# RMSNorm with doubled rows: wide squares, sums on VectorE, powers on GpSimd

## The chip, the cores and the metric

The kernel runs on one core of one Trainium2 chip. The metric is device microseconds of that core; a measurement is a median over several runs. Engines are named as in the profile: DVE is VectorE, ACT is ScalarE, POOL is GpSimd, SP is SyncE, which here only issues DMAs. Rows of the profile that end in q (SPq) belong to an engine's queue of waits and DMA issues.

## What is computed

```python
B, S, D = 8, 512, 2048
x_rep = np.repeat(x, 2, axis=1)
rms = np.sqrt((x_rep ** 2).mean(axis=-1, keepdims=True) + 1e-6)
out = ((x_rep / rms) * gamma[None, None, :]).astype(np.float32)
```

Each row of 2048 float32 numbers is divided by its root mean square, multiplied by gamma, and written twice. 33.56 MB are read and 67.11 MB written.

## The kernel before

The 4096 rows are cut into 8 tiles. A tile `y` has 128 partitions with K = 4 rows of x each, and room for 8 rows (R = 2 output rows for each row of x). The load puts the 4 rows of x into slots 4 to 7 of the tile; the results go in place into slots 0, 2, 4, 6, and copies of them into slots 1, 3, 5, 7. The store then writes all 8 slots, 64 KB for a partition. There are three buffers of this kind, so a load of tile 3 needs the store of tile 0 to be done, and so on.

Per row `k` of a tile, `square` (L64, L68) makes ScalarE square the row into PSUM with the row's sum in an accumulator, and take the root of its mean plus eps. `scale` (L73, L74) makes VectorE take the reciprocal and multiply row, reciprocal and the broadcast gamma in one instruction (scalar_tensor_tensor). After four rows `repeat` (L81) copies the first two results on ScalarE and the last two on VectorE, both at once 4096 elements wide.

The order is written out by hand: each engine runs its instructions in the order of the program. SP issues all loads (L52) and stores (L56) of tiles on one queue, in this order: load 0 in two halves, loads 1, 2; stores 0, 1, 2; loads 3, 4, 5; stores 3, 4; loads 6, 7; stores 5, 6, 7. The lines that set this:

```python
loads_after = {2: (3, 4, 5), 4: (6, 7)}
for i in range(ntiles):
    compute(i)
    store(i, 0, K)
    for j in loads_after.get(i, ()):
        load(j, nc.sync)
```

Gamma is read in seven pieces by ScalarE's queue (L95) into one partition, and GpSimd broadcasts it to all 128 (L96).

Of the kernel before, what the change touches and what calls it, by code (L numbers as in the profile page):

```python
# [1 line left out]

# [4 lines left out]


@with_exitstack
def kernel(  # L10
    ctx: ExitStack,
    tc: tile.TileContext,
    x: bass.AP,
    gamma: bass.AP,
    out: bass.AP,
):
    nc = tc.nc
    P = nc.NUM_PARTITIONS
    f32 = mybir.dt.float32
    Act = mybir.ActivationFunctionType  # L20
    Alu = mybir.AluOpType

    B, S, D = x.shape
    Bo, So, Do = out.shape
    R = So // S
    assert R == 2 and D == Do and B == Bo and So == S * R
    eps = 1e-6
    inv_d = 1.0 / float(D)


    K = 4
    N = B * S
    assert N % (P * K) == 0
    ntiles = N // (P * K)
    x_t = x.rearrange("b s d -> (b s) d").rearrange("(n p k) d -> n p k d", p=P, k=K)
    out_t = out.rearrange("b s d -> (b s) d").rearrange("(n p j) d -> n p (j d)", p=P, j=K * R)

    singles = ctx.enter_context(tc.tile_pool(name="singles", bufs=1))
    rows = ctx.enter_context(tc.tile_pool(name="rows", bufs=3))
    junk = ctx.enter_context(tc.tile_pool(name="junk", bufs=1, space=bass.MemoryType.PSUM))  # L40
    small = ctx.enter_context(tc.tile_pool(name="small", bufs=8))

    ys = []

    def load(i, eng, parts=1):


        y = rows.tile([P, K * R, D], f32, name="y")
        step = K // parts
        for k in range(0, K, step):  # L50
            at = K * (R - 1) + k
            eng.dma_start(out=y[:, at : at + step, :], in_=x_t[i, :, k : k + step, :])  # L52
        ys.append(y)

    def store(i, k0, k1):
        nc.sync.dma_start(  # L56
            out=out_t[i, :, R * k0 * D : R * k1 * D],
            in_=ys[i][:, R * k0 : R * k1, :].rearrange("p j d -> p (j d)"),
        )

    def square(i, k):
        sq = junk.tile([P, D], f32, name="sq")
        ss = small.tile([P, 1], f32, name="ss")
        nc.scalar.activation(  # L64
            out=sq[:], in_=ys[i][:, K * (R - 1) + k, :], func=Act.Square, accum_out=ss[:]
        )
        rms = small.tile([P, 1], f32, name="rms")
        nc.scalar.activation(out=rms[:], in_=ss[:], func=Act.Sqrt, scale=inv_d, bias=eps_t[:])  # L68
        return rms

    def scale(i, k, rms):
        rstd = small.tile([P, 1], f32, name="rstd")
        nc.vector.reciprocal(out=rstd[:], in_=rms[:])  # L73
        nc.vector.scalar_tensor_tensor(  # L74
            out=ys[i][:, R * k, :], in0=ys[i][:, K * (R - 1) + k, :], scalar=rstd[:], in1=gamma_b[:],
            op0=Alu.mult, op1=Alu.mult,
        )

    def repeat(i, k0, k1, copy):
        y_r = ys[i].rearrange("p (k r) d -> p k r d", r=R)  # L80
        copy(out=y_r[:, k0:k1, 1, :], in_=y_r[:, k0:k1, 0, :])  # L81

    def compute(i):
        for k in range(K):
            scale(i, k, square(i, k))
        repeat(i, 0, K // 2, nc.scalar.copy)
        repeat(i, K // 2, K, nc.vector.tensor_copy)


    ctx.enter_context(tc.manual_schedule())  # L90
    load(0, nc.sync, parts=2)
    gamma_b = singles.tile([P, D], f32, name="gamma_b")
    cuts = [0, *range(D // 4, D + 1, D // 8)]
    for c0, c1 in zip(cuts, cuts[1:]):
        nc.scalar.dma_start(out=gamma_b[0:1, c0:c1], in_=gamma[c0:c1].partition_broadcast(1))  # L95
    nc.gpsimd.partition_broadcast(out_ap=gamma_b[:], in_ap=gamma_b[0:1, :])  # L96
    eps_t = singles.tile([P, 1], f32, name="eps_t")
    nc.vector.memset(eps_t, eps)  # L98
    load(1, nc.sync)
    load(2, nc.sync)  # L100

    assert ntiles == 8
    loads_after = {2: (3, 4, 5), 4: (6, 7)}
    for i in range(ntiles):
        compute(i)
        store(i, 0, K)
        for j in loads_after.get(i, ()):
            load(j, nc.sync)  # L110


# [1 line left out]
_INS = ['x', 'gamma']  # L114
_OUTS = [((8, 1024, 2048), 'float32')]


# [23 lines left out]
```

## Time and profile before

| | |
|---|---|
| median of 3 runs | 239.44 us (239.32 to 239.5) |
| the profiled execution's own time | 239.72 us |
| its span, first to last instruction | 237.9 us |
| busy DVE / ACT / POOL | 96.5 / 101.0 / 2.5 us |
| main DMA queue q1 | 100.66 MB, 98.5% of 16 engines' span |
| DMA over the span | 423 GB/s |
| stores issued at | 27.05, 39.22, 51.39, 115.86, 128.25, 160.08, 184.02, 196.41 us |
| first x instruction of tiles 0, 3, 6 on ACT | 8.12, 101.18, 169.34 us |

Times in the trace are microseconds from the start of the span. A row of a group of instructions gives line, engine, operation, output<-input with partitions x elements and type, then xcount, then busy us, the mean ns of one instruction, and the idle time of the engine just before them with what ended most of it. A row of waits gives who waited for whom, us in total, how often, and the longest. A busy share of a DMA queue near 100% says that its 16 engines had packets all the time.

### The profile page before, as it was taken

The page shows a single profiled execution, that of the slowest core. Times are in us where ns is not written, and L with a number is a line of the kernel's source. Part 1 is how long each engine was busy: PE and PEld are TensorE (multiplying, and loading weights), DVE is VectorE, ACT ScalarE, POOL GpSimd, SP SyncE. Part 2 cuts the span into 40 slices and gives each one's busy share as a digit, 9 for nine tenths or more (in the row PEclk, how much of TensorE's full clock was granted, in tenths as well). Part 3 has the DMA queues.
Part 4 walks back from the last instruction along what each step waited for, and adds up shares of the span by engine and source line. Part 5 has one row for each costly group of instructions (what it writes and reads, how often), then busy time and mean ns, then how long its engine had stood idle before and what let it go on. Part 6 is the DMA issues. An engine that isn't in the chain of part 4 may idle for free.

```text
span 237.9 us, 287 instructions
## 1 busy us (share of the span) xinstructions
DVE 96.5 (41%) x73; ACT 101.0 (42%) x106; POOL 2.5 (1%) x5
## 2 busy tenths in 40 slices
DVE  0049999960000000059999960000199990000000
ACT  2697999900000000099999920000599960000000
POOL 0030000000000000000000000000000000000000
DMA  7999998989899998999998999989998989999994
GB/s 265 436 446 441 441 441 353 530 353 496 386 452 430 397 485 353 441 441 441 441 518 364 464 419 430 452 369 430 435 518 364 518 364 485 397 452 430 408 474 176
DMA packets 2464, 100.69 MB, mean 423 GB/s; under 512 B 279, under 2 KB 285, under 8 KB 286
## 3 DMA queue, kind: packets, MB, share of 16 engines
q1 hardware_dynamic: 2448, 100.66, 98.5%
q14 instruction: 2, 0.02, 0.0%
q10 hardware_dynamic: 14, 0.01, 0.0%
HBM read 33.56 MB, written 67.11 MB: 423 GB/s over the span
## 4 chain that ended last, share of the span: by engine, by line
DMA 58%; ACT 12%; DVE 9%; issue 1%; POOLq 1%; ACTq 1%; SPq 0%
DMA y<-in_x_dram 33%; DMA out_dram<-y 21%; ACT sq L64 8%; DVE y L74 7%; DMA gamma_b<-in_gamma_dram 4%; ACT y L81 3%; DVE y L81 2%; ACT rms L68 1%; POOLq L136 1%; ACTq L95 1%; DVE rstd L73 0%; POOLq L96 0%; SPq L56 0%
## 5 line engine op out<-in xcount | busy, mean ns | idle before, releaser
L64 ACT ACTIVATE sq<-y 128x2048 f32<-128x2048 f32 x32 | 59.7, 1865 | 87.8 <-DMA y<-in_x_dram 87.8
L74 DVE SCALAR_TENSOR_TENSOR y<-y,rstd,gamma_b 128x2048 f32<-128x2048 f32 x32 | 75.3, 2352 | 4.1 <-POOL gamma_b L96 3.0
L73 DVE RECIPROCAL rstd<-rms 128x1 f32<-128x1 f32 x32 | 5.0, 158 | 94.6 <-ACT rms L68 94.3
L81 ACT COPY y<-y 128x4096 f32<-128x4096 f32 x8 | 28.7, 3590 | 1.4 <-DVE y L74 1.4
L81 DVE COPY y<-y 128x4096 f32<-128x4096 f32 x8 | 18.3, 2294 | 0.3
L68 ACT ACTIVATE rms<-ss,eps_t 128x1 f32<-128x1 f32 x32 | 9.4, 295 | 1.0
L64 ACT ACTIVATION_READ_ACCUMULATOR sq<-y 128x1 f32 x32 | 6.0, 187 | 0.0
L64 ACT ACT_TABLE_LOAD x1 | 1.3, 1283 | 3.0 <-issue 3.0
L96 POOL PARTITION_BROADCAST gamma_b<-gamma_b x1 | 2.3, 2294 | 12.2 <-DMA y<-in_x_dram 12.2
L68 ACT ACT_TABLE_LOAD x1 | 1.3, 1283 | 0.0
L98 DVE MEMSET eps_t<- 128x1 f32 x1 | 0.1, 59 | 0.8 <-PEq L125 0.8
L125 POOL MEMSET const-uint8-127<- 128x1 uint8 x1 | 0.1, 102 | 0.0
L125 POOL MEMSET const-bfloat16-1.0<- 128x1 bf16 x1 | 0.1, 101 | 0.0
L125 POOL MEMSET const-float32-0.0<- 128x1 f32 x1 | 0.1, 98 | 0.2 <-issue 0.2
L125 POOL MEMSET const-float32-1.0<- 128x1 f32 x1 | 0.1, 98 | 0.0
## 6 DMA issues: line engine op xcount, KB each, us to landing
y<-in_x_dram SPq DMA_DIRECT2D x7, 4096.0 KB, 14.6
y<-in_x_dram SPq DMA_DIRECT2D x2, 2048.0 KB, 7.4
out_dram<-y SPq DMA_DIRECT2D x8, 24.4
gamma_b<-in_gamma_dram ACTq DMA_DIRECT2D x6, 1.0 KB
gamma_b<-in_gamma_dram ACTq DMA_DIRECT2D x1, 2.0 KB
```

Source lines behind the costliest of these rows:

```text
L64: nc.scalar.activation(out=sq[:], in_=ys[i][:, K * (R - 1) + k, :], func=Act.Square, accum_out=ss[:])
L68: nc.scalar.activation(out=rms[:], in_=ss[:], func=Act.Sqrt, scale=inv_d, bias=eps_t[:])
L73: nc.vector.reciprocal(out=rstd[:], in_=rms[:])
L74: nc.vector.scalar_tensor_tensor(out=ys[i][:, R * k, :], in0=ys[i][:, K * (R - 1) + k, :], scalar=rstd[:], in1=gamma_b[:], op0=Alu.mult, o ...
L81: copy(out=y_r[:, k0:k1, 1, :], in_=y_r[:, k0:k1, 0, :])
L95: nc.scalar.dma_start(out=gamma_b[0:1, c0:c1], in_=gamma[c0:c1].partition_broadcast(1))
L96: nc.gpsimd.partition_broadcast(out_ap=gamma_b[:], in_ap=gamma_b[0:1, :])
L98: nc.vector.memset(eps_t, eps)
L125: nc = _bacc.Bacc("TRN2", target_bir_lowering=False, num_devices=1)
L136: with _tile.TileContext(nc) as tc:
```

## The change

- Tiles 1, 4 and 6 ("mixed"): ScalarE squares rows 1 to 3 in one wide instruction into slots 1 to 3 of the tile, and row 0 as before with its accumulated sum; VectorE sums the three squared rows with one tensor_reduce. Tiles 2, 5 and 7: all four rows are squared in one wide instruction, which stands in ScalarE's order ahead of the copies of the tile before, and VectorE sums all four.
- The root of these six tiles is taken on GpSimd for four rows at once: a multiply and add (mean plus eps), then a power of -0.5.
- Tiles 0 and 3 keep a root on ScalarE and a reciprocal on VectorE, two rows at a time. Tile 0's last two rows are squared in one wide instruction and summed on VectorE; tile 3's rows are all summed by ScalarE's accumulator.
- Tile 5 is scaled row by row on ScalarE by the reciprocal root, and multiplied by gamma in one instruction over four rows on VectorE; all its copies are one ScalarE instruction. Tile 7's copies are both on ScalarE.
- Gamma's seven pieces are issued by SP: six between the two halves of load 0, one after them. They land in two partitions, and GpSimd broadcasts each half by itself.
- eps and the exponents are set by GpSimd, and ScalarE's table for the root is loaded at the start. The order of loads and stores of tiles on SP is as before.

```diff
+    def total(i, k, ss):
         sq = junk.tile([P, D], f32, name="sq")
-        ss = small.tile([P, 1], f32, name="ss")
         nc.scalar.activation(
-            out=sq[:], in_=ys[i][:, K * (R - 1) + k, :], func=Act.Square, accum_out=ss[:]
-        )
-        rms = small.tile([P, 1], f32, name="rms")
-        nc.scalar.activation(out=rms[:], in_=ss[:], func=Act.Sqrt, scale=inv_d, bias=eps_t[:])
-        return rms
+            out=sq[:], in_=ys[i][:, x_at + k, :], func=Act.Square, accum_out=ss[:, k : k + 1]
+        )
+
+    def square(i, k0, k1):
+        nc.scalar.activation(
+            out=ys[i][:, k0:k1, :], in_=ys[i][:, x_at + k0 : x_at + k1, :], func=Act.Square
+        )
+
+    def reduce(i, k0, k1, ss):
+        nc.vector.tensor_reduce(
+            out=ss[:, k0:k1], in_=ys[i][:, k0:k1, :], op=Alu.add, axis=mybir.AxisListType.X
+        )
+
+    def root(k0, k1, ss):
+        at = ss[:, k0:k1]
+        nc.gpsimd.tensor_scalar(
+            out=at, in0=at, scalar1=inv_d, scalar2=eps, op0=Alu.mult, op1=Alu.add
+        )
+        nc.gpsimd.tensor_tensor(out=at, in0=at, in1=power_t[:, k0:k1], op=Alu.pow)
...
+    nc.scalar.preload_act_table(Act.Sqrt)
+    load(0, 0, H)
+    for c0, c1 in zip(cuts[:-2], cuts[1:-1]):
+        gamma_piece(c0, c1)
+    load(0, H, K)
+    gamma_piece(cuts[-2], cuts[-1])
+    for c0 in (0, D // 2):
+        nc.gpsimd.partition_broadcast(out_ap=gamma_b[:, c0 : c0 + D // 2], in_ap=gamma_half(c0))
+    load(1, 0, K)
+    load(2, 0, K)
...
+    def root_quick(k0, k1, ss):
+        at = ss[:, k0:k1]
+        nc.scalar.activation(out=at, in_=at, func=Act.Sqrt, scale=inv_d, bias=eps_t[:])
+        nc.vector.reciprocal(out=at, in_=at)
+
+    ss = columns()
+    for k in range(H):
+        total(0, k, ss)
+    root_quick(0, H, ss)
+    ss_b = columns()
+    between = ys[0].rearrange("p (k r) d -> p k r d", r=R)[:, 0:H, 1, :]
+    nc.scalar.activation(
+        out=between, in_=ys[0][:, x_at + H : x_at + K, :], func=Act.Square
+    )
+    scale(0, 0, H, ss)
+    nc.vector.tensor_reduce(
+        out=ss_b[:, H:K], in_=between, op=Alu.add, axis=mybir.AxisListType.X
+    )
+    root_quick(H, K, ss_b)
+    repeat(0, 0, H)
+    scale(0, H, K, ss_b)
+    repeat(0, H, K, nc.vector.tensor_copy)
+    store(0)
+
+    def mixed(i, ahead=None, last=nc.vector.tensor_copy, row=True):
+        ss = columns()
+        if row:
+            square(i, 1, K)
+            total(i, 0, ss)
+            reduce(i, 1, K, ss)
+        else:
+            reduce(i, 0, K, ss)
+        root(0, K, ss)
+        if ahead is not None:
+            square(ahead, 0, K)
+        scale(i, 0, K, ss)
+        repeat(i, 0, H)
+        repeat(i, H, K, last)
+        store(i)
+
+    mixed(1, ahead=2)
+    mixed(2, row=False)
+    for j in (3, 4, 5):
+        new_tile()
+        load(j, 0, K)
+    ss = columns()
+    for k in range(H):
+        total(3, k, ss)
+    root_quick(0, H, ss)
+    scale(3, 0, H, ss)
+    ss_b = columns()
+    for k in range(H, K):
+        total(3, k, ss_b)
+    root_quick(H, K, ss_b)
+    scale(3, H, K, ss_b)
+    repeat(3, 0, H)
+    repeat(3, H, K, nc.vector.tensor_copy)
+    store(3)
+    mixed(4, ahead=5)
...
+    reduce(5, 0, K, ss)
+    root(0, K, ss)
+    for k in range(K):
+        nc.scalar.activation(
+            out=ys[5][:, R * k, :], in_=ys[5][:, x_at + k, :], func=Act.Copy, scale=ss[:, k : k + 1]
+        )
+    y_r = ys[5].rearrange("p (k r) d -> p k r d", r=R)
+    nc.vector.tensor_tensor(
+        out=y_r[:, :, 0, :], in0=y_r[:, :, 0, :],
+        in1=gamma_b[:].rearrange("p (k d) -> p k d", k=1).to_broadcast([P, K, D]), op=Alu.mult,
+    )
+    repeat(5, 0, K)
+    store(5)
+    mixed(6, ahead=7)
+    mixed(7, row=False, last=nc.scalar.copy)
```

## The prediction

> **What bounds the kernel now.** I read the busy times first, then the DMA lines, then what the DMA-issuing engine SP waits for, then the groups of instructions.
>
> From the page, busy time by engine, the DMA share of 40 slices, and the share of the main DMA queue:
>
> ```profile
> DVE 96.5 (41%) x73; ACT 101.0 (42%) x106; POOL 2.5 (1%) x5
> ...
> DMA  7999998989899998999998999989998989999994
> ...
> q1 hardware_dynamic: 2448, 100.66, 98.5%
> ```
>
> No engine is half busy, while q1 fills 98.5% of the span: the kernel is a stream of 100.66 MB. By stages, 0 to 2 us moves 91 GB/s, 232 to 234 us still 492, 234 to 236 only 33. Data thus runs from about 1.7 us (an estimate: the first load is issued at 0.72) to 234.2 us, 433 GB/s. A 4.19 MB load is then 9.7 us of stream, an 8.39 MB store 19.4.
>
> What SP waited for (us in total, times, longest):
>
> ```profile
> SPq L56 <- DVE y L81: 108.8, 7, 23.9
> SPq L52 <- DMA out_dram<-y: 69.6, 5, 19.1
> ```
>
> SP issues all loads and stores of x and out in one order, and each store (L56) waits for the last copy of its tile on VectorE. Such a wait is free while the queue still holds work. Whether it does is read from the issue times: stores at 27.05, 39.22, 51.39, 115.86, 128.25, 160.08, 184.02, 196.41 us. The stream reaches their data (1.7 us plus all bytes ahead at 433 GB/s) at 30.8, 50.2, 69.5, 118.0, 137.3, 176.1, 195.5, 214.8. Every store is early, but store 0 by 3.7 us and store 3 by 2.1 us only. **A store issued later than its turn, less its start-up, stops the stream, and that time never comes back.**
>
> The groups that price the change (busy, mean ns | idle before):
>
> ```profile
> L64 ACT ACTIVATE sq<-y 128x2048 f32<-128x2048 f32 x32 | 59.7, 1865 | 87.8 <-DMA y<-in_x_dram 87.8
> L74 DVE SCALAR_TENSOR_TENSOR y<-y,rstd,gamma_b 128x2048 f32<-128x2048 f32 x32 | 75.3, 2352 | 4.1 <-POOL gamma_b L96 3.0
> L73 DVE RECIPROCAL rstd<-rms 128x1 f32<-128x1 f32 x32 | 5.0, 158 | 94.6 <-ACT rms L68 94.3
> L81 ACT COPY y<-y 128x4096 f32<-128x4096 f32 x8 | 28.7, 3590 | 1.4 <-DVE y L74 1.4
> L81 DVE COPY y<-y 128x4096 f32<-128x4096 f32 x8 | 18.3, 2294 | 0.3
> L68 ACT ACTIVATE rms<-ss,eps_t 128x1 f32<-128x1 f32 x32 | 9.4, 295 | 1.0
> L64 ACT ACTIVATION_READ_ACCUMULATOR sq<-y 128x1 f32 x32 | 6.0, 187 | 0.0
> ```
>
> Per tile VectorE has 4 x 2.35 + 4 x 0.16 + 2.29 = 12.3 us, against 19.4 us of store: 7 us to spare.
>
> **What the Trainium skill says.** "VectorE: DVE Perf Modes", the perf-mode tier table: tensor_reduce has a 1x program only, an fp32 copy runs at 2x. Its side-by-side section gives a fixed part of about 150 cycles at 0.96 GHz. The trace agrees on the copy: (4096/2 + 150)/0.96 = 2290 ns against 2294; the trace has no reduction. "ScalarE: Activation LUTs", What ACT_TABLE_LOAD costs: 186 ns + 0.833 ns an element; for 4096 that is 3598 ns, the copy here takes 3590. "GPSIMD Engine Reference", 3.1: about 2.6 cycles an element for tensor_tensor plus two software dispatches; neither it nor the trace has a power.
>
> **The change part by part.** Added prices, as estimates from these: reduction of 2, 3 and 4 rows (4096+150)/0.96 = 4.42, 6.56, 8.69 us; wide square of 3 rows 5.31, of 4 rows 7.01 us on ScalarE. One dependent scale to the next is 2.39 (2.35 and a 0.04 hand-over, as between 22.30 and 24.69 us). Start-up of a store on an empty queue: the first load was issued at 0.72, landed after 7.4 us and holds 4.84 us of stream; 2.56 us lie around it, I put 1.0 of them ahead of the data (0.6 to 1.4). **The root on GpSimd**, two dependent instructions on 128x4: a memset of 128x1 took 0.10 us, the two need dispatch, a power in software and two semaphores; I take 1.0 us, with 0.3 (three memsets) and 2.0 (near the 2.29 us of the broadcast) as ends. It can't gain: VectorE's next instruction needs it.
>
> Removed on ScalarE, per mixed tile: three accumulator reads and all root activations, and for tiles 2, 5, 7 all four reads. At 42% busy and idle before its loads this is worth nothing. Removed on VectorE: 0.16 us reciprocals. Added there: the sums. A mixed tile costs VectorE 6.56 + 1.0 + 9.56 + 2.30 = 19.4 us, one without the row on ScalarE 8.69 + 1.0 + 9.56 + 2.30 = 21.6, against the store's 19.4. **The 7 us to spare are gone**, and VectorE and the stream run at one pace. The walk:
>
> Tile 0. Gamma: seven small DMAs move from ScalarE's queue to SP's. Six are issued behind the first half load (6 x 0.27 us, so the second half at about 3.0 us, needed at 6.5: hidden). The seventh waits for the first half's landing at 8.1, and the loads of tiles 1 and 2 behind it on SP follow at about 8.5 and 8.9, as now. It lands behind the second half load at about 13; half a broadcast is 2.29/2 = 1.15: gamma at 14.3 (13.7 to 15.5) instead of 14.92. The earlier table load saves 1.28 us on ScalarE, hidden behind gamma. VectorE: two scales to 19.1, reduction to 23.5, root on ScalarE and reciprocal to 24.0, two scales to 28.8, copy to 31.1. Data at 32.1; the loads end at 30.8: **1.4 late**.
>
> Tile 1. ScalarE copies tile 0's half to 27.4, squares three rows to 32.7 (one row with its own sum by 34.8, beside the reduction). Reduction to 39.3, root 40.3, scales 49.9, copy 52.2, data 53.2; store 0 ends at 51.5: **1.7 late**.
>
> Tile 2. Its square is ready at 41.8. 21.6 more: issue 73.7, data 74.7, store 1 ends at 72.6: **2.2 late**. The three loads behind it on SP wait for their buffers' stores anyway (as in SP's second row), and the stream still has them in time.
>
> Tile 3. Load 3 lands at 94.1 + 9.7 + 1.6 = 105.4. Two row totals 4.2, root 0.5, two scales 4.8 (ScalarE does the other totals meanwhile), two scales 4.8 after a reciprocal, copy 2.3: 16.8 after landing against 14.7 now (101.18 to 115.86). Data at 123.2, loads 4 and 5 end at 123.2: 0.
>
> Tile 4. Square ends at 123.8 on ScalarE, reduction 130.4, root 131.4, scales 140.9, copy 143.2, data 144.2; store 3 ends 142.6: **1.7 late**. Load 6 waits behind this store on SP, but needs store 3's landing anyway.
>
> Tile 5. Sum 151.9, root 152.9, four scales on ScalarE (1.9 each) 160.6, the product by gamma on VectorE at 1x (8.69) 169.3, one copy of 8192 on ScalarE 176.5. The cover is loads 6 and 7, which end at 183.0: hidden, but ScalarE is late for tile 6.
>
> Tile 6. Square 181.8, sum 188.4, root 189.4, scales 198.9, copy 201.2, data 202.2; store 5 ends 202.4: 0, just.
>
> Tile 7. Sum 209.9, root 210.9, scales 220.5, second half copied on ScalarE 3.6: 224.1, data 225.1; store 6 ends 221.7: **3.3 late**.
>
> **Sum:** 1.4 + 1.7 + 2.2 + 1.7 + 3.3 = 10.3 us of empty stream. The profiled execution has a span of 237.9 and took 239.72, so 248.2 and 250.0; the median of the runs is 0.28 below it: **249.7 us**. One microsecond more or less per root counts in tiles 1, 2, 4, 5, 6 and 7, six times, while stores are late. Root 0.3 with a start-up of 0.6 gives 5.3 us of gaps (244.7); root 2.0 gives 16.3 (255.7). A reduction some 5% cheaper takes about 2 us off the low end.
>
> **The rivals.** *Cheap sums, no change.* If a reduction took three quarters of the price or less (6.5 us for 4 rows), the gaps would fall to 0.5 us with roots of 1.0: 239.4 to 239.9. For it: no reduction in the trace. Against it: the price table, whose copy row the trace confirms to 4 ns. *Dear power, much slower.* GpSimd at 3 us a root gives 22.3 us of gaps, 261.7. For it: a power in software that nothing here prices; against it: only four elements a partition. *Cleaner start, faster.* Gamma's pieces leave the second queue (14 packets of q10 today), where they share DMA engines with the first load; the first 8 us move 2.4 MB where 433 GB/s from 1.7 us would move 2.7. If the pieces in SP's own queue gave back 0.3 MB, 0.7 us, and the sums were so cheap that no store is late, the time would be 238.7. It decides only where all gaps together are under 0.7 us, and the first load's issue at 0.72 doesn't move; so it needs the first rival too. That the change doesn't do what it says I exclude: the instruction order of each engine shows the sums on VectorE and six pairs on GpSimd.
>
> **How the numbers follow.** About 0.2% (0.48 us) is what a measurement of this kernel can tell from no change. Forecast (VectorE's chain paces the stores) 0.80, dear power 0.04, cheap sums 0.12, cleaner start 0.04. So faster 0.04, same 0.12, slower 0.84. The range is the forecast's own, 243 to 256, which leaves 0.20 outside.
>
> **What would show it.** DVE TENSOR_REDUCE rows near 4.4, 6.6 and 8.7 us; GpSimd's pair about 1 us from the sum's end to the next scale; VectorE over 60% busy; store issues near 31, 52, 74, 122, 143, 177, 201, 224 us; q1 down to about 94% of the span, with dents in the DMA row near 31, 52, 74, 143 and 224 us. It is wrong if the reductions are well under these prices, or if q1 stays at 98% of its span.

## The result, and the profile after

The changed kernel takes 248.82 us (median of 6 runs, 248.33 to 249.09) against 239.35 us before in the same runs: ratio 1.0393, 95% interval 1.038 to 1.0407, 9.5 us slower. Forecast were 249.7 us and a range of 243 to 256. The profiled execution took 248.60 us with a span of 246.8, which is 8.9 us more than the 237.9 of before.

The page of the changed kernel, busy time, DMA by slices and the main queue:

```profile
DVE 137.6 (56%) x46; ACT 103.7 (42%) x43; POOL 10.2 (4%) x20
...
DMA  7999989969779796999997979899999979797893
...
q1 hardware_dynamic: 2462, 100.67, 95.9%
```

ScalarE's busy time hardly moved (101.0 to 103.7), VectorE's rose by 41 us, and the queue that was full is no longer full: the row has sixes and sevens where the row of before has nines and eights. A digit doesn't place a gap to the microsecond, as a store's packets are long; the issue times below do.

The groups that cost it, kept apart by shape (line, engine, operation | busy, mean ns | idle before and its releaser):

```profile
L87 DVE SCALAR_TENSOR_TENSOR y<-y,ss,gamma_b 128x2048 f32<-128x2048 f32 x28 | 64.8, 2349 | 9.9 <-POOL ss L83 7.4 <-POOL gamma_b L131 2.2
L74 DVE TENSOR_REDUCE ss<-y 128x4 f32<-128x8192 f32 x3 | 26.0, 8677 | 0.0
...
L74 DVE TENSOR_REDUCE ss<-y 128x3 f32<-128x6144 f32 x3 | 19.7, 6553 | 15.5 <-ACT y L69 15.5
...
L83 POOL TENSOR_TENSOR ss<-ss,power_t 128x4 f32<-128x4 f32 x6 | 6.1, 1016 | 0.5
L156 DVE TENSOR_REDUCE ss<-y 128x2 f32<-128x4096 f32 x1 | 4.4, 4411 | 0.0
...
L80 POOL TENSOR_SCALAR ss<-ss 128x4 f32<-128x4 f32 x6 | 1.2, 194 | 189.4 <-DVE ss L74 189.4
```

The four-row sums of tiles 2 and 7 start with no idle before them: VectorE goes from one tile straight into the next. Tile 2 in order of time (start, us), from the last copy of tile 1 to its own:

```profile
50.30 2.29 DVE L94 COPY y<-y 128x4096 f32<-128x4096 f32 x1
52.51 8.68 DVE L74 TENSOR_REDUCE ss<-y 128x4 f32<-128x8192 f32 x1
52.66 0.34 SPq L56 DMA_DIRECT2D out_dram<-y  x1
61.28 0.19 POOL L80 TENSOR_SCALAR ss<-ss 128x4 f32<-128x4 f32 x1 [20.31 <-DVE ss L74]
61.55 1.01 POOL L83 TENSOR_TENSOR ss<-ss,power_t 128x4 f32<-128x4 f32 x1
62.60 9.27 DVE L87 SCALAR_TENSOR_TENSOR y<-y,ss,gamma_b 128x2048 f32<-128x2048 f32 x4 [1.41 <-POOL ss L83]
67.30 3.60 ACT L94 COPY y<-y 128x4096 f32<-128x4096 f32 x1 [17.99 <-DVE y L87]
71.90 2.29 DVE L94 COPY y<-y 128x4096 f32<-128x4096 f32 x1
```

From copy to copy 21.6 us, and store 1 (issued at 52.66) needs 19.4 us of stream. The chain that ended last is now one of engines, not of DMAs; its end (start, us, what):

```profile
210.89 1.06 POOLq L244
211.94 0.03 issue
211.97 6.89 DVE y L87 x3
218.86 0.02 issue
218.88 2.36 DVE y L87
221.25 0.02 issue
221.27 3.60 ACT y L94
```

It is tile 7: power on GpSimd, four scales, copy on ScalarE; the store followed at 224.90. All stores, in us:

| store | issued before | forecast | issued after | its turn | late | engines empty |
|---|---|---|---|---|---|---|
| 0 | 27.05 | 31.1 | 31.47 | 30.8 | 0.7 | 0.5 |
| 1 | 39.22 | 52.2 | 52.66 | 50.9 | 1.8 | 1.7 |
| 2 | 51.39 | 73.7 | 74.26 | 72.1 | 2.2 | 2.2 |
| 3 | 115.86 | 122.2 | 122.23 | 122.8 | 0 | 0 |
| 4 | 128.25 | 143.2 | 143.57 | 142.2 | 1.4 | 0.6 |
| 5 | 160.08 | 176.5 | 177.12 | 182.4 | 0 | 0 |
| 6 | 184.02 | 201.2 | 202.03 | 201.8 | 0.3 | 0 |
| 7 | 196.41 | 224.1 | 224.90 | 221.4 | 3.5 | 2.1 |

"Its turn" is reckoned: the last late store's issue plus 19.4 us for each store and 9.7 for each load in between (30.8 for store 0, as in the forecast). "Engines empty" is measured, from the starts and ends of the DMA packets in the trace: the time without a packet ahead of that store, as a mean of the 16 DMA engines. In the kernel before it is under 0.1 us in all between 20 us and the end of the stream.

The engines were empty for 7.1 us. Each of the five stores that let the stream run dry has its first packet 0.83 to 0.85 us after its issue: this is its start-up. The reckoned lateness (9.8 us in all) is too much for stores 4, 6 and 7. Store 6 was not late at all: its first packet starts 19.3 us after that of store 5, as in the full stream of before.

The second part of the loss is slower packets: on the mean of the 16 engines, store packets took 1.8 us and load packets 0.5 us more in all than in the kernel before. Most of it, 1.4 us, is the last store packet of each engine ahead of load 3 and ahead of load 6: 2.8 to 3.5 us in place of 2.42. Ahead of load 3 these slow packets stand in all nine runs whose stream had run dry before, and in none of the other five; why, no run here shows. Together the engines end 9.3 us later on the mean; as they end within 0.2 us of each other, where those of before spread over 1.4 us, the last one ends 8.5 us later (245.3 against 236.8).

### The profile page after: what moved, and what is told of

It reads as the page before. It is cut to its first block, busy times and chain, and to the rows that moved or that the text cites. A ratio compares the mean times of both kernels' runs of the same rounds, so it can differ in the third digit from the quotient of the medians.

```text
span 246.8 us, 223 instructions
## 1 busy us (share of the span) xinstructions
DVE 137.6 (56%) x46; ACT 103.7 (42%) x43; POOL 10.2 (4%) x20
## 3 DMA queue, kind: packets, MB, share of 16 engines
q1 hardware_dynamic: 2462, 100.67, 95.9%
## 5 line engine op out<-in xcount | busy, mean ns | idle before, releaser
L87 DVE SCALAR_TENSOR_TENSOR y<-y,ss,gamma_b 128x2048 f32<-128x2048 f32 x28 | 64.8, 2349 | 9.9 <-POOL ss L83 7.4
L94 ACT COPY y<-y 128x4096 f32<-128x4096 f32 (+1 forms) x9 | 35.8, 3982 | 56.8 <-DVE y L87 48.0
L74 DVE TENSOR_REDUCE ss<-y 128x3 f32<-128x6144 f32 (+1 forms) x6 | 45.7, 7615 | 15.5 <-ACT y L69 15.5
L69 ACT ACTIVATE y<-y 128x6144 f32<-128x6144 f32 (+1 forms) x6 | 37.0, 6168 | 1.4 <-DMA y<-in_x_dram 1.4
L63 ACT ACTIVATE sq<-y 128x2048 f32<-128x2048 f32 x9 | 16.9, 1872 | 41.0 <-DMA y<-in_x_dram 40.9
L94 DVE COPY y<-y 128x4096 f32<-128x4096 f32 x6 | 13.8, 2293 | 0.2
L211 DVE TENSOR_TENSOR y<-y,gamma_b 128x8192 f32<-128x8192 f32 x1 | 8.7, 8693 | 9.3 <-ACT y L207 9.3
L207 ACT ACTIVATE y<-y,ss 128x2048 f32<-128x2048 f32 x4 | 7.8, 1994 | 13.3 <-POOL ss L83 13.3
L83 POOL TENSOR_TENSOR ss<-ss,power_t 128x4 f32<-128x4 f32 x6 | 6.1, 1016 | 0.5
L156 DVE TENSOR_REDUCE ss<-y 128x2 f32<-128x4096 f32 x1 | 4.4, 4411 | 0.0
```

The source lines that it names most:

```text
L63: nc.scalar.activation(out=sq[:], in_=ys[i][:, x_at + k, :], func=Act.Square, accum_out=ss[:, k : k + 1])
L69: nc.scalar.activation(out=ys[i][:, k0:k1, :], in_=ys[i][:, x_at + k0 : x_at + k1, :], func=Act.Square)
L74: nc.vector.tensor_reduce(out=ss[:, k0:k1], in_=ys[i][:, k0:k1, :], op=Alu.add, axis=mybir.AxisListType.X)
L83: nc.gpsimd.tensor_tensor(out=at, in0=at, in1=power_t[:, k0:k1], op=Alu.pow)
L87: nc.vector.scalar_tensor_tensor(out=ys[i][:, R * k, :], in0=ys[i][:, x_at + k, :], scalar=rstd[:, k : k + 1], in1=gamma_b[:], op0=Alu.mul ...
L156: nc.vector.tensor_reduce(out=ss_b[:, H:K], in_=between, op=Alu.add, axis=mybir.AxisListType.X)
```

## The experiments

Each was timed beside the kernel before; ratios are to its runs in the same session, with 95% intervals. The short diffs are against the changed kernel or the kernel before, as said.

**Sums back on ScalarE** (against the changed kernel).

```diff
-            square(i, 1, K)
-            total(i, 0, ss)
-            reduce(i, 1, K, ss)
-        else:
-            reduce(i, 0, K, ss)
+            for k in range(K):
+                total(i, k, ss)
...
-            square(ahead, 0, K)
+            for k in range(K):
+                total(ahead, k, sums[ahead])
...
```

> The changed kernel, with the sums of tiles 1, 2, 4, 5, 6, 7 taken again by ScalarE's accumulator, row by row; GpSimd's roots, gamma by halves, tile 0, tile 3 and tile 5's scaling on ScalarE stay. Theory (VectorE's chain of sum, root, scales and copy paces the stores): without the sum the chain is 1.45 + 9.3 + 2.3 = 13.1 us a tile against 19.4 of store, so only store 0 (issued at 31.47, 0.7 us past its turn) can cost: 239.4 to 240.2 us, store 1 issued near 49, store 7 well before 200. Rival A (the root on GpSimd is dear by itself) and rival B (gamma's seven DMAs on SP disturb the start): it stays above 244.

240.61 us, 1.0053 (1.0038 to 1.0068). Of the 9.5 us, 8.2 are gone with the sums (and the wide squares that feed them), though the six GpSimd roots, gamma's halves and tile 5 on ScalarE are all there. Stores 1 and 7 are issued at 48.73 and 205.07. The median is 0.4 us above what I expected; what is left is taken apart under "Sums on ScalarE, with that change later".

**Roots on ScalarE and VectorE, sums as changed.**

```diff
-        nc.gpsimd.tensor_scalar(
-            out=at, in0=at, scalar1=inv_d, scalar2=eps, op0=Alu.mult, op1=Alu.add
-        )
-        nc.gpsimd.tensor_tensor(out=at, in0=at, in1=power_t[:, k0:k1], op=Alu.pow)
+        nc.scalar.activation(out=at, in_=at, func=Act.Sqrt, scale=inv_d, bias=eps_t[:])
+        nc.vector.reciprocal(out=at, in_=at)
```

> The changed kernel with the six roots taken by a ScalarE activation and a VectorE reciprocal instead of two GpSimd instructions; the sums stay on VectorE. Theory: the step from the sum's end to the next scale falls from 1.41-1.60 to about 0.6 us; a microsecond per root counts six times, so about 5.2 us less: 243.6 us (242.8 to 244.4). Still slower than before, since sums stay. Rival (the GpSimd root is the whole cost): 239.4. Rival (the sums alone, roots hidden): 248.8.

243.70 us, 1.0177 (1.016 to 1.0194), as expected. Its tile 2 in order of time:

```profile
51.51 8.68 DVE L74 TENSOR_REDUCE ss<-y 128x4 f32<-128x8192 f32 x1
...
60.22 0.30 ACT L80 ACTIVATE ss<-ss,eps_t 128x4 f32<-128x4 f32 x1 [10.05 <-DVE ss L74]
60.55 0.18 DVE L81 RECIPROCAL ss<-ss 128x4 f32<-128x4 f32 x1 [0.36 <-ACT ss L80]
60.77 9.26 DVE L85 SCALAR_TENSOR_TENSOR y<-y,ss,gamma_b 128x2048 f32<-128x2048 f32 x4
```

From the sum's end (60.19) to the scale 0.58 us, against 1.41 above.

**A second power after each root.**

```diff
         nc.gpsimd.tensor_tensor(out=at, in0=at, in1=power_t[:, k0:k1], op=Alu.pow)
+        nc.gpsimd.tensor_tensor(out=at, in0=at, in1=one_t[:, k0:k1], op=Alu.pow)
...
```

> The changed kernel with a second power (exponent 1) after each of the six roots on GpSimd: one more instruction of 1.02 us, 1.1 us with its hand-over. Theory: counts six times while stores are late, 6.6 us more: 255.4 us (254.5 to 256.3). Rival (the stores are late for another reason and the root is hidden): 248.8. Rival (only the tiles whose store is late now count, 5 of them): 254.0 or less.

255.18 us, 1.0656 (1.064 to 1.0672): 6.36 us more than the changed kernel for six instructions. The added one of tile 2 and the scale behind it:

```profile
63.51 1.01 POOL L84 TENSOR_TENSOR ss<-ss,one_t 128x4 f32<-128x4 f32 x1
64.55 9.26 DVE L88 SCALAR_TENSOR_TENSOR y<-y,ss,gamma_b 128x2048 f32<-128x2048 f32 x4 [2.49 <-POOL ss L84]
```

The wait grew from 1.41 to 2.49, by 1.08; 6 x 1.08 = 6.5. With the run before it, the dose goes both ways: about a microsecond of time for a microsecond in each of the six roots, tile 5's included although its own store is early, because ScalarE and then tiles 6 and 7 come later with it (the next run shows that path).

**Tile 5 on VectorE.**

```diff
-    reduce(5, 0, K, ss)
-    root(0, K, ss)
-    for k in range(K):
-        nc.scalar.activation(
...
-    repeat(5, 0, K)
-    store(5)
+    mixed(5, row=False)
```

> The changed kernel with tile 5 computed as tile 2 is (scales and half of the copies on VectorE) instead of scaled on ScalarE with one product and one wide copy. Theory: store 5 is early either way; ScalarE comes free earlier, so tile 6's square starts at its load's landing (about 174.3) and not at 177.0; its sum ends 2.7 us earlier, store 6 is no longer late and store 7 less late by the same: 246.0 us (245.3 to 247.0). Rival (scaling on ScalarE relieves VectorE and pays): slower, 249 to 253, since VectorE gets 9.3 + 2.3 us in place of 8.7.

246.76 us, 1.0305 (1.0289 to 1.032), 2.1 us less than the changed kernel. Scaling tile 5 on ScalarE, the one part that spares VectorE work (8.69 us of product for 9.3 + 2.3), costs time: ScalarE is held until 177.0 and tile 6's square waits for it. Without it, that square waits for its load alone:

```profile
175.66 5.32 ACT L69 ACTIVATE y<-y 128x6144 f32<-128x6144 f32 x1 [13.31 <-DMA y<-in_x_dram]
```

**Two rows on each engine.**

```diff
-            square(i, 1, K)
-            total(i, 0, ss)
-            reduce(i, 1, K, ss)
-        else:
-            reduce(i, 0, K, ss)
+            square(i, H, K)
+            for k in range(H):
+                total(i, k, ss)
+        reduce(i, H, K, ss)
...
-            square(ahead, 0, K)
+            square(ahead, H, K)
+            for k in range(H):
+                total(ahead, k, sums[ahead])
...
```

> The changed kernel with the rows shared: in tiles 1, 2, 4, 5, 6, 7 rows 0 and 1 summed by ScalarE's accumulator, rows 2 and 3 squared in one wide instruction and summed on VectorE. Theory (a pace): VectorE's chain is 4.41 + 1.45 + 9.3 + 2.3 = 17.5 us, under the store's 19.4, so no store but store 0 (0.7 us) can be late: 239.4 to 240.3 us. Rival (each sum on VectorE costs time in proportion): half of the added time stays, near 244.

240.96 us, 1.006 (1.0046 to 1.0073). Half of the sums on VectorE, and not half of the 9.5 us but 1.4 us are left: it is a pace that must be kept, not a cost in proportion. It is 0.7 us above the expected upper end. Its store 0 was issued at 32.14, 1.3 us past its turn; by the packets the engines were empty for 0.8 us there, and slower store packets took 0.9 us more than in the kernel before.

**The roots alone on GpSimd** (against the kernel before).

```diff
-        for k in range(K):
-            scale(i, k, square(i, k))
+        if i in (0, 3):
+            for k in range(K):
+                scale(i, k, square(i, k))
+        else:
...
+            nc.gpsimd.tensor_scalar(
+                out=ss[:], in0=ss[:], scalar1=inv_d, scalar2=eps, op0=Alu.mult, op1=Alu.add
+            )
+            nc.gpsimd.tensor_tensor(out=ss[:], in0=ss[:], in1=power_t[:], op=Alu.pow)
...
```

> The kernel before with only the roots of tiles 1, 2, 4, 5, 6, 7 moved to GpSimd, four rows at once; sums stay in ScalarE's accumulator, gamma on ScalarE's queue. Theory: VectorE's chain is 13.1 us, stores stay early by several us: 239.4 us, within 0.2%. Rival (GpSimd's root costs by itself): 6 x 1.3 us more, 247.

242.46 us, 1.0123 (1.0105 to 1.014). **My theory failed here.** No store is late: they are issued at 27.16, 45.40, 63.07, 117.97, 136.90, 162.43, 192.97 and 210.62 us. Nor do the roots count one by one. But load 3 lands 2.1 us later than before (tile 3's first square at 103.28 against 101.18), with no store late ahead of it. "One GpSimd instruction" below takes this up.

**Gamma alone** (against the kernel before).

```diff
...
-    for c0, c1 in zip(cuts, cuts[1:]):
-        nc.scalar.dma_start(out=gamma_b[0:1, c0:c1], in_=gamma[c0:c1].partition_broadcast(1))
-    nc.gpsimd.partition_broadcast(out_ap=gamma_b[:], in_ap=gamma_b[0:1, :])
...
+    for c0, c1 in zip(cuts[:-2], cuts[1:-1]):
+        gamma_piece(c0, c1)
...
+    gamma_piece(cuts[-2], cuts[-1])
+    for c0 in (0, D // 2):
+        nc.gpsimd.partition_broadcast(out_ap=gamma_b[:, c0 : c0 + D // 2], in_ap=gamma_half(c0))
```

> The kernel before with only gamma's loading changed: seven pieces on SP's queue around the second half load, two partitions, two half broadcasts. Theory: first scale at about 14.8 us as now, store 0 still early: 239.4 us, within 0.2%. Rival (cleaner start): up to 0.7 us less. Rival (SP is held up by the seventh piece and the stream runs dry): some us more.

239.48 us, 0.9998 (0.999 to 1.0007): no difference. So gamma's halves and SP's wait for the seventh piece have no part in the 9.5 us. (The run above kept gamma as it was before, so they can't be its cause either.)

**No arithmetic** (against the kernel before).

```diff
-        for k in range(K):
-            scale(i, k, square(i, k))
-        repeat(i, 0, K // 2, nc.scalar.copy)
-        repeat(i, K // 2, K, nc.vector.tensor_copy)
+        h = K // 2
+        nc.scalar.copy(out=ys[i][:, 0:h, :], in_=ys[i][:, K : K + h, :])
+        nc.vector.tensor_copy(out=ys[i][:, h:K, :], in_=ys[i][:, K + h : 2 * K, :])
```

> The kernel before with the arithmetic left out: squares, roots and scales are gone, each tile only has its four rows of x copied to the other four slots, half on ScalarE and half on VectorE, and the same loads and stores in the same order (the output is not the norm). Theory (the stream of 100.66 MB bounds the kernel before): 239.4 us, within 0.3%: nothing that the engines do in the kernel before is on the clock. Rival (engines are part of its time): several us less.

239.12 us, 0.9982 (0.9974 to 0.9991), with VectorE busy for 20.1 us in place of 96.5. All the arithmetic of the kernel before is worth 0.4 us; what remains is the stream. None of the versions tried that compute the norm beats the kernel before, and with this order of loads and stores there is little to win.

**One GpSimd instruction** (against the kernel before), to take apart what the roots alone had cost. In all kernels above with arithmetic on GpSimd after the broadcast, the program has one more GpSimd instruction between the two, which the views above leave out. In the trace of this run its records stand at 15.0 us under the name MODIFY_POOL_CONFIG; the kernel before has such records only at 0.8 us, ahead of the broadcast.

```diff
+    spare = singles.tile([P, K], f32, name="spare")
+    nc.gpsimd.memset(spare, 1.0)
+    nc.gpsimd.tensor_scalar(
+        out=spare[:], in0=spare[:], scalar1=inv_d, scalar2=eps, op0=Alu.mult, op1=Alu.add
+    )
```

> The kernel before plus one small GpSimd instruction (multiply and add on 128x4 of a tile that nobody reads) after the broadcast of gamma. In the kernels so far that have GpSimd arithmetic after the broadcast, the program puts an unnamed instruction (a change of GpSimd's program library) between the two, and load 3 landed later than the late stores explain: 103.28 us with the roots alone on GpSimd against 101.18, with no store late. Theory C (that change, at about 15 to 22 us, holds up loads that are in flight): 240.5 to 242.5 us with all other work as before. Rival (the roots themselves, later, cost the time): 239.4.

242.53 us, 1.0119 (1.0106 to 1.0132): one instruction of 0.19 us that nobody waits for costs as much as the six roots did (242.46). GpSimd's timeline of this run:

```profile
12.72 2.30 POOL L96 PARTITION_BROADCAST gamma_b<-gamma_b  x1 [12.29 <-DMA y<-in_x_dram]
14.86 0.21 POOL L100 MEMSET spare<- 128x4 f32 x1
27.05 0.19 POOL L101 TENSOR_SCALAR spare<-spare 128x4 f32<-128x4 f32 x1 [11.97 <-issue]
```

12 us pass between memset and arithmetic in which the profile shows nothing ("issue"). I read that, with the record's name, as a change of GpSimd's program. In the DMA packets of that trace, seven of loads 1 and 2, started at 19.9 to 21.6 us, took 1.5 to 2.1 us instead of the usual 1.21 for 32 KB. All eight kernels that make this change at about 15 us have such packets at 17 to 22 us (2 to 8 of them); the kernel before has none in that time, nor have the kernels above without GpSimd arithmetic (roots on ScalarE, gamma alone, no arithmetic). The end of the stream then frays, here in windows of 2 us (last two columns: DMA share and GB/s; a packet counts in the window in which it starts), first this run, then the kernel before:

```profile
234.00:236.00 2.00, 0.00 (x0) 0.00 (x0) 0.00 (x0) 1.00 0.45 197
236.00:238.00 2.00, 0.00 (x0) 0.00 (x0) 0.00 (x0) 1.00 0.30 131
```

```profile
234.00:236.00 2.00, 0.00 (x0) 0.00 (x0) 0.00 (x0) 1.00 0.08 33
236.00:238.00 2.00, 0.00 (x0) 0.00 (x0) 0.00 (x0) 1.00 0.00 0
```

By the ends of their packets the 16 DMA engines finish between 235.8 and 239.6 us here, between 235.4 and 236.8 in the kernel before. A packet of a store takes 2.42 us in both traces, so an engine that has fallen behind in a full queue has no way to catch up: put in sequence, the packets have the slowest engine about 2.4 us behind at 33 us and still 2.4 at 150.

**The roots alone, with that change later** (against the roots alone).

```diff
+                if i == 1 and k == 2:
+                    gate = singles.tile([P, 1], f32, name="gate")
+                    nc.scalar.copy(out=gate[:], in_=eps_t[:])
+                    nc.gpsimd.memset(gate, 0.0)
```

> The kernel before with the six roots on GpSimd, as measured at 242.46 us, but GpSimd first waits for ScalarE's third square of tile 1 (a one-column copy on ScalarE, a one-column memset on GpSimd), so that the change of library falls at about 30 us, when the first three loads are all but done and a store is in the queue. Theory C: no load is held up, 239.4 to 239.9 us. Rival C2 (it holds up stores as it does loads): stays at 241 to 243. Rival (the roots themselves): 242.5.

243.05 us, 1.0149 (1.0129 to 1.0168): as a time inconclusive, by a fault of the experiment. I had reckoned with a short change of program. It took 9.3 us here (GpSimd's memset at 29.64, arithmetic at 39.08), the first root came after it, and store 1 was issued at 52.18, 2.0 us past its turn of 50.2. Load 3 landed 2.0 us later than before, as that store explains. The packets tell what the time can't. With the change moved to 29.8 us, no load packet started at 15 to 24 us took more than 1.21 us (eight took 1.4 to 2.5 without the gate), and no store packet started at 28 to 42 us took more than 2.42. The engines finish between 238.4 and 240.0 us, without the gate between 236.2 and 240.2. So the slow loads go with the change of program, and stores in flight were not held up by it (rival C2). The even end can come from this or from the empty stretch at store 1. That the time would then be that of the kernel before is not shown: the late store 1 left the engines empty for 0.9 us, and slower packets took 0.9 us (stores) and 1.2 us (loads, most of it at 116 to 121 us, cause open) more than in the kernel before.

**Sums on ScalarE, with that change later** (against the first experiment).

```diff
+                if i == 1 and k == 0:
+                    gate = singles.tile([P, 1], f32, name="gate")
+                    nc.scalar.copy(out=gate[:], in_=eps_t[:])
+                    nc.gpsimd.memset(gate, 0.0)
```

> The changed kernel with all sums of tiles 1, 2, 4, 5, 6, 7 on ScalarE's accumulator (measured at 240.61 us), and GpSimd waiting for tile 1's first square before its library changes, at about 30 us. Theory C: what is left is tile 0's late store (31.3 us, 0.5 us past its turn): 239.5 to 240.0 us. Rival (all of the rest is store 0's lateness): 240.6.

241.04 us, 1.0054 (1.0041 to 1.0066), against 1.0053 without the gate: no gain. Store 0 was issued at 31.98 here, 0.7 us later than without the gate (31.28), as the first load had landed later (first square at 8.62 against 8.03). The packets part the two effects. Without the gate the engines are empty for 0.3 us at store 0, and store packets took 0.8 us more than in the kernel before; with it these are 0.9 and 1.1 us, while load packets took 0.3 us less and none at 15 to 24 us is slow. So what is left of the first experiment is store 0's lateness and the slower store packets after it. What the change of program adds there is about 0.3 us of load packets.

**All second copies on ScalarE** (against the changed kernel).

```diff
-    def mixed(i, ahead=None, last=nc.vector.tensor_copy, row=True):
+    def mixed(i, ahead=None, last=nc.scalar.copy, row=True):
```

> The changed kernel with the copies of rows 2 and 3 in tiles 1, 2, 4 and 6 on ScalarE instead of VectorE. Theory (a pace, not a latency): the store waits for a copy of 3.6 us instead of 2.3, so store 1 and store 4 are 1.3 us later, but VectorE starts each next sum 2.3 us earlier: 19.45 us a tile instead of 21.6. Store 2 near 73.4, store 7 near 220.5: 245.0 to 246.0 us. Rival (the chain from sum to store within a tile decides): 1.3 us later at each of four stores, 250 to 254.

247.32 us, 1.0323 (1.0308 to 1.0338), 1.5 us less than the changed kernel. The direction is the pace's, the stores came where expected (store 1 at 53.89, 2 at 73.16, 7 at 220.96), but the time is 1.3 us above the range. Store 7 no longer let the stream run dry: its first packet starts 19.3 us after that of store 6. The engines are empty for 5.2 us in place of 7.1, and slower packets cost about as much as in the changed kernel (2.2 us for 2.3). I had counted store 7's lateness as 3.5 us, of which the packets show only 2.1; that is about the 1.3 us.

## Why the prediction was right, point by point

**Right: the bound and the mechanism.** The stream bounds the kernel before: shown by the run without arithmetic. VectorE's chain took over the pace: shown by sums taken away (8.2 us back), halved (7.9 back), roots shortened (5.1 back) and lengthened (6.4 more). All eight stores were issued within 0.9 us of the walk.

**Right: the prices of the sums.** "VectorE: DVE Perf Modes" of the Trainium skill, perf-mode tier table, has tensor_reduce at 1x for fp32, and with the fixed part of about 150 cycles of the page's side-by-side section I had 4.42, 6.56 and 8.69 us; measured are 4.41, 6.55 and 8.68. The product over four rows measured 8.69, as estimated. The wide squares, by "ScalarE: Activation LUTs", What ACT_TABLE_LOAD costs, took 5.32 and 7.02 us for 5.31 and 7.01.

**Off in size, in opposite ways, and near by luck.** The root was put at 1.0 us, and the step from sum to scale took 1.41 to 1.60 (0.19 for the multiply, 1.02 for the power, the rest hand-overs): too low by 0.4 to 0.6, six times. Four scales in a row took 9.27, not 9.56: the 2.39 us was read from a scale and the copy that needs its result, and the scales of a tile don't need each other. So the stores came up to 0.8 us later than forecast.

The turns were reckoned too early. I took 234.2 us for the end of the data from windows that count a packet where it starts, and a store packet lasts 2.42 us; by its packets the stream of before ended between 235.4 and 236.8. Store 0's first packet started at 32.42 for 30.8 reckoned, store 7's at 216.06 for 214.8. With that, the forecast 10.3 us of empty stream was 7.1: stores 0, 4 and 7 had been put at 1.4, 1.7 and 3.3 us and left 0.5, 0.6 and 2.1. The start-up of 1.0 us (0.6 to 1.4) was right in size: 0.84. In no term of the walk are the slower packets, 2.3 us more. They made up for most of what the empty stream had been put too high, and 249.7 would not have been so near 248.8 without them. Two of the signs were off too: VectorE was 56% busy, not over 60%, and q1 stood at 95.9%, not about 94%.

**Right: the parts costed at nothing.** Gamma by halves changed nothing by itself (0.9998); the first scale started at 14.83 against 14.92, where I had 14.3, as the broadcast of a half took 1.30 us and not 1.15. Tile 5's store stayed early (177.12 for a turn of 182.4), and that it was late for tile 6 through ScalarE is shown by the run with tile 5 on VectorE.

**Missed: what comes with GpSimd arithmetic.** The prediction priced the two GpSimd instructions of a root and put the change of program between broadcast and arithmetic at nothing, as it did not name it. In a kernel with a full stream it costs 2.9 us. In the changed kernel it did not add to the sum: the run with roots on ScalarE, which has no such instruction, lost 5.1 us, about what the six shorter steps alone are worth (6 x 0.83 to 1.0). That the empty stretches let the slow DMA engines catch up would explain it, and the engines of the changed kernel do end within 0.2 us of each other (245.1 to 245.3); no run takes it by itself.

**The rivals.** Cheap sums and dear power fall by the measured rows (8.68 and 1.02 us). The cleaner start falls by the run with gamma alone.

## What to carry to other kernels

In a kernel bounded by one queue of transfers, write down for each store when its turn comes and when it is issued; an engine's work is free up to that difference, and from there every microsecond counts, in each later tile whose store is late too. The end of a transfer is read from its packets, not from a view that counts them where they start. Fewer and wider instructions are no gain if they move work to the engine whose chain releases the stores: here 4 rows summed in one 8.7 us instruction replaced work that another engine had done for nothing. An operation on an engine that had been used for one thing only can bring hidden work along, so try a single instruction of it by itself.

## What the runs showed that I had not expected

- One small GpSimd multiply-and-add after a partition broadcast made the kernel before 2.9 us slower (242.53 against 239.65), with 12.0 us of GpSimd in which the profile shows nothing; in the two runs with a gate it was 9.3 and 5.3 us. "GPSIMD Engine Reference" of the Trainium skill, 2.1, says that the first call to a freshly loaded kernel pays about 6 us with no visible instruction; here the time without a visible instruction was up to twice that. Loads in flight are slower meanwhile: the slow packets at 17 to 22 us are gone where a gate moved the change or no change was made. How the one acts on the other, no run shows.
- The power of GpSimd on 128x4 numbers takes 1.02 us, with either exponent tried, five times the 0.19 us of a multiply and add.
- In every run whose DMA engines had stood empty before, the last store packet of each engine ahead of load 3 took up to 3.6 us instead of 2.42, which is 0.6 to 0.8 us on the mean of the engines; in no other run did it. The cause is open.
